# Two late gates of a decoder trunk: z times (1 + tanh(z/2)), halved later, in place of z times sigmoid(z)

## The chip, the cores and the metric

The kernel runs on one core of a Trainium2 chip. The metric is the device time of one execution in microseconds (us). Four compute engines work side by side, each with its own queue that is executed in order: TensorE (PE: matmuls and transposes), VectorE (DVE), ScalarE (ACT: copies, casts and activation functions) and GpSimd (POOL). SyncE (SP) only issues transfers here. Engines wait for one another through semaphores. Matmul results land in PSUM, everything else is in SBUF.

## The reference

A decoder trunk of one layer, for 1024 tokens of width 1024, all in float32: three groups of attention heads side by side, an output projection, a gated MLP with a convolution, a gated embedding and a last norm. The change touches the third group, retention, whose output is gated:

```
def _retention(q, k, v, g, cos, sin):
    ...
    o = _unchunk(o)
    o = _rmsnorm(o) * jax.nn.silu(g.astype(jnp.float32))
    return o.reshape(b, s, -1)
```

silu(g) is g times sigmoid(g). The first group (HGRN2) gates its output in the same way. The second group, attention in a window of 128 tokens, needs exponentials for its softmax.

## The kernel before, in words

Every matmul of float32 operands is split into high and low parts: `mm3` (lines 113 to 117) issues three matmuls, on lines 115, 116 and 117. `split_w` makes the two parts of a weight tile: ACT casts the high part (line 102), the engine named by `e` subtracts to get the low part (line 104).

The input projection has 22 column tiles of 128 columns. `project` computes one of them: a tile is a pair of PSUM banks, one for each half of the tokens (`z_cg` and the like, tag `g`, three banks in all). A function `post` then takes the two banks to SBUF, which frees them. `mixed_in` interleaves, in program order, the steps of one head group with those of the projections that follow, and the tile framework's scheduler orders each engine's queue from that program by priorities and its own estimates; so a changed instruction can move others.

The last such stage is the windowed attention (`window`, 32 steps: four pairs of heads i, two heads hd of a pair, four steps of two token blocks). A step has three pieces. `first`: score matmuls (`sb`, lines 605 and 606), masks (609, 610), the maximum (612, 613), two exponentials on ACT with their sum (line 617, tiles `pr` and `bden`). `second`: two transposes of the exponentials (`tb`, line 625), a copy of them on ACT (627) and a masked copy on DVE (628), both into `pT`. `third`: products with the values (`pob`, lines 640 and 641); at the last step of a head the sums are completed (`es` 646, `bden` 647, 648) and the output scaled (649). `heads` prepares the queries of a pair (`qs`: a cast on ACT, line 748, a subtraction on DVE, line 749).

Beside this stage run the last five projections, named in LATE: bq1, bq2, bq3 and the two retention gates cg0 and cg1. Their post for the gates is `gate` (lines 313 to 319): line 290 scales a bank by the row norms into `cg` in SBUF, ACT writes sigmoid(cg) back into the freed bank (317), DVE multiplies the two (318), and after that the bank is free. The two gates of the first head group, ag0 and ag1, went the same way in earlier stages, where no exponentials are computed.

ACT holds one set of function tables at a time. Where an activation needs another set, an instruction ACT_TABLE_LOAD stands before it. In this stage exponentials and sigmoids alternate.

The first two tiles of the output projection (`o`, `out_tile_half`, lines 823 to 827) already start in this stage; they need PSUM banks of the same tag `g`, the second one the bank of the first half of cg1. Their first operands are `ha` and `la`, the high and low part of the first group's gated output: `split` casts `ha` on ACT (line 379), and GpSimd subtracts to `la` (line 380). Both go into buffers that the projection's inputs held, so they wait until PE has used those inputs in cg1.

After the stage, `gated` turns each retention output by transposes (`gc`) and multiplies it with its gate (line 392 without a gain, line 394 with a column of gains, as for the first head group), and `split` makes the two parts `hc` and `lc`.

Of the kernel before, what the change touches and what calls it, by code (L numbers as in the profile page):

```python
# [21 lines left out]
AF = mybir.ActivationFunctionType  # L22
ALU = mybir.AluOpType
# [19 lines left out]
LATE = ("bq1", "bq2", "bq3", "cg0", "cg1")  # L43
# [30 lines left out]
def trunk(ctx: ExitStack, tc: tile.TileContext, a, out, out_end, dbg):  # L74
    nc = tc.nc
    V, S, G, TE = nc.vector, nc.scalar, nc.gpsimd, nc.tensor
# [6 lines left out]
    def dump(name, t):  # L83
        if name in dbg:
            nc.sync.dma_start(dbg[name], t.bitcast(F32) if t.dtype == F32R else t)

    def pg(name):
        return ps.tile([P, H2], F32, tag="g", bufs=3, name=name)

    def b1(name):  # L90
        return ps.tile([P, H2], F32, tag="b1", bufs=5, name=name)

    def half(h):
        return slice(h * H2, (h + 1) * H2)
# [112 lines left out]
    pt = b1("idle")  # L207
# [3 lines left out]
    with tc.high_priority(offset=100000):  # L211
# [4 lines left out]
        for k in range(KD):  # L216
# [10 lines left out]
            for h in range(2):  # L227
                S.mul(hi[:, half(h)], x[:, half(h)], col(C_G1 + k))
                V.scalar_tensor_tensor(out=lo[:, half(h)], in0=x[:, half(h)], scalar=col(C_G1 + k),
                                       in1=hi[:, half(h)].bitcast(F32), op0=ALU.mult, op1=ALU.subtract)  # L230
# [57 lines left out]
    def scaled(dst, o):  # L288
        for h in range(2):
            V.tensor_tensor(out=dst[:, half(h)], in0=o[h], in1=rs1[:, half(h)], op=ALU.mult)  # L290

    def zt(name, tag, bufs):
        return ap.tile([P, T], F32, tag=tag, bufs=bufs, name=name)

    def plain(o, name, tag, bufs):
        t = zt(name, tag, bufs)
        scaled(t, o)
        return t

    def transposed(src, name, evac):  # L300

        for h in range(2):
            pt = b1(f"{name}{h}")
            for c in range(4):
                TE.transpose(pt[:, chunk(c)], src[:, chunk(h * 4 + c)], ident)
            evac(h, pt.rearrange("p (c d) -> p c d", c=4))
# [5 lines left out]

    def gate(o, name):

        g = plain(o, name, "zg", 4)
        for h in range(2):
            S.activation(o[h], g[:, half(h)], AF.Sigmoid)
            V.tensor_tensor(out=g[:, half(h)], in0=o[h], in1=g[:, half(h)], op=ALU.mult)
        return g
# [54 lines left out]
    def split(src, gain, name, e=V, parts=1):  # L374
        hi, lo = [big.tile([P, T], F32R, tag="big", name=x + name) for x in "hl"]
        for i in range(parts):
            c = slice(i * T // parts, (i + 1) * T // parts)
            if gain is None:
                S.copy(hi[:, c], src[:, c])
                e.tensor_tensor(out=lo[:, c], in0=src[:, c], in1=hi[:, c].bitcast(F32), op=ALU.subtract)  # L380
            else:
                S.mul(hi[:, c], src[:, c], gain)
                V.scalar_tensor_tensor(out=lo[:, c], in0=src[:, c], scalar=gain, in1=hi[:, c].bitcast(F32),
                                       op0=ALU.mult, op1=ALU.subtract)
        return hi, lo

    def gated(zo, g, gain, name):

        def evac(h, pt):
            gv = g[:, half(h)].rearrange("p (c d) -> p c d", c=4)  # L390
            if gain is None:
                V.tensor_tensor(out=gv, in0=pt, in1=gv, op=ALU.mult)
            else:
                V.scalar_tensor_tensor(out=gv, in0=pt, scalar=gain, in1=gv, op0=ALU.mult, op1=ALU.mult)
        transposed(zo.rearrange("p c d -> p (c d)"), "g" + name, evac)
        dump("mix" + name, g)
        return g
# [12 lines left out]
    def hgrn_f(j, of):  # L410
        f = zt(f"f{j}", "zf", 1)
        k = zt(f"k{j}", "zk", 2)
        scaled(f, of)
        S.activation(k, f, AF.Sigmoid, scale=-1.0)
        S.activation(f, f, AF.Sigmoid)
        V.tensor_scalar(out=k, in0=k, scalar1=oml[:, j:j + 1], scalar2=None, op0=ALU.mult)
        V.tensor_scalar(out=f, in0=f, scalar1=oml[:, j:j + 1], scalar2=lbt[:, j:j + 1], op0=ALU.mult, op1=ALU.add)
        return f, k
# [244 lines left out]
    def window_out(i, zo):  # L663
        hi = big.tile([P, T], F32R, tag="big", name=f"hmb{i}")
        lo = big.tile([P, T], F32R, tag="big", name=f"lmb{i}")

        def evac(h, pt):
            pt = pt.rearrange("p c d -> p (c d)")
            S.copy(hi[:, half(h)], pt)
            V.tensor_tensor(out=lo[:, half(h)], in0=pt, in1=hi[:, half(h)].bitcast(F32), op=ALU.subtract)  # L670
        transposed(zo.rearrange("p c d -> p (c d)"), f"mb{i}", evac)
        dump(f"mixb{i}", hi)
        return hi, lo
# [4 lines left out]
    got = {}  # L678
# [16 lines left out]
    def gates(n):  # L695
        return keep(n, lambda o: gate(o, n))

    def out_tile(n, tag="zo"):
        return ap.tile([P, NC, P], F32, tag=tag, bufs=1, name=n)
# [6 lines left out]
    def mix_tile(name, z, gate, gain):  # L706

        mix[name] = gated(z, got[gate], gain, name)
        yield 0.9

    v = plain(first[2], "ai0", "zt", 1)
    f, k = hgrn_f(0, first[0])
# [5 lines left out]
    f, k = got["af1"]  # L718
# [5 lines left out]
    zc = [out_tile(f"oc{j}", ("zo", "zF")[j]) for j in range(2)]  # L724
# [34 lines left out]
             tiles_of(rot("bq1", "zq"), rot("bq2", "zq"), rot("bq3", "zq"), gates("cg0"), gates("cg1")), 0.82, 8.0)  # L759
    mh = [split(mix[n], None, n, G) for n in ("a0", "a1")]  # L760
    mh += [window_out(i, zb[i]) for i in range(4)]
    mh += [split(gated(zc[j], got[f"cg{j}"], None, f"c{j}"), None, f"c{j}") for j in range(2)]
    att.__exit__(None, None, None)
    fp = ctx.enter_context(tc.tile_pool(name="ffn", bufs=1))
    dp = ctx.enter_context(tc.tile_pool(name="spill", bufs=1, space=bass.MemoryType.DRAM))
# [103 lines left out]
    for n, (h, i, d) in enumerate((h, i, d) for h in range(2) for i in range(2) for d in range(4)):  # L869
        hi, lo = wpp[i]  # L870
        o = pg(f"pp{n}")
# [319 lines left out]
    got = {}  # L1191
    bank = {}
    todo = []
    for n, (i, j) in enumerate(steps):
# [14 lines left out]
        if j == NJ - 1:  # L1209
            d0, h = TO[i]  # L1210
# [23 lines left out]
    c = half(0)  # L1234
# [37 lines left out]
    for n in range(NC // 2):  # L1272
# [7 lines left out]
        for i, (d0, d1) in enumerate(groups):  # L1280
# [4 lines left out]
            o = pg(f"pe{n}{i}")[:, :d1 - d0]  # L1285
# [12 lines left out]
            else:  # L1298
                V.scalar_tensor_tensor(out=v[:, 3:4], in0=v[:, i:i + 1], scalar=1.0 / D, in1=v[:, 3:4],
                                       op0=ALU.mult, op1=ALU.add)  # L1300
# [3 lines left out]
        if not last:  # L1304
# [6 lines left out]
                               op1=ALU.mult)  # L1311
# [116 lines left out]
```

## Time and profile before

| | |
|---|---|
| median of three runs | 1246.35 us (1245.96 to 1246.54) |
| the profiled execution, own time | 1246.38 us |
| its span, first to last instruction | 1244.6 us |
| PE busy | 1225.4 us (98%) |
| DVE busy | 892.2 us (72%) |
| ACT busy | 543.8 us (44%) |
| POOL busy | 126.7 us (10%) |

The span is that of the profiled execution; 1.8 us of its own time lie outside it. The shares are means over the whole program. PE's matmuls are pipelined: each is listed with 0.39 us, but the next starts about 0.23 us after it, so the starts tell more than the durations.

### The profile page before, as it was taken

What the parts mean: (1) busy time and instruction counts of PE and PEld (TensorE: products, weight loads), DVE (VectorE), ACT (ScalarE), POOL (GpSimd) and SP (SyncE); (2) the same over time, 40 slices, a digit from 0 to 9 for tenths busy, and PEclk for the clock granted to TensorE, in tenths of its full rate; (3) what the DMA queues carried; (4) which work ended last, traced back from release to release, by engine and by line L of the source; (5) the groups of instructions that cost most, each with busy time, mean ns of one, the idle gap of its engine ahead of it and who ended that gap; (6) DMA issues with size and microseconds to landing.
All of it is one profiled execution on the core that took longest, in us unless ns stands there. A gap on an engine that the chain in (4) does not pass through costs nothing.

```text
span 1244.6 us, 15889 instructions
## 1 busy us (share of the span) xinstructions
PE 1225.4 (98%) x6030; PEld 1023.5 (82%) x6030; DVE 892.2 (72%) x1510; ACT 543.8 (44%) x838; POOL 126.7 (10%) x158
## 2 busy tenths in 40 slices
PE   9999999999999999999999999999999999999997
PEld 7888888887888888887788888888888888888886
DVE  7996967557777476987878887787667675566374
ACT  7324233247766344754343334433335353444332
POOL 2000000011210313100111111111101000000000
PEclk9999999999999999999999999999999999999999
DMA  7100110110001944333554544544579786443131
GB/s 258 51 23 29 35 34 18 34 34 34 24 29 46 353 127 166 121 94 127 177 177 152 179 130 154 182 160 154 191 265 339 272 290 207 144 152 119 34 135 68
DMA packets 59964, 165.53 MB, mean 133 GB/s; under 512 B 6320, under 2 KB 6832, under 8 KB 59888
## 3 DMA queue, kind: packets, MB, share of 16 engines
q1 hardware_dynamic: 42608, 106.71, 25.6%
q0 software_dynamic: 15552, 55.84, 13.2%
q10 hardware_dynamic: 1728, 1.97, 0.5%
q8 instruction: 47, 0.77, 0.3%
q14 instruction: 29, 0.24, 0.1%
HBM read 120.20 MB, written 44.30 MB: 132 GB/s over the span
## 4 chain that ended last, share of the span: by engine, by line
PE 51%; DVE 1%; DMA 0%; issue 0%; ACT 0%; DVEq 0%
PE d L116 6%; PE d L115 6%; PE d L117 6%; PE gb L116 5%; PE gb L117 5%; PE gb L115 5%; PE gd L117 3%; PE gd L115 3%; PE gd L116 3%; PE ga L116 1%; PE ga L117 1%; PE ga L115 1%; PE pe L117 1%; PE pg L115 1%; PE pe L115 1%; PE pe L116 1%
## 5 line engine op out<-in xcount | busy, mean ns | idle before, releaser
L115 PE MATMUL d<-hhd,hwd 128*128 128x512 f32 x308 | 119.8, 389 | 0.0
L116 PE MATMUL d<-lhd,hwd 128*128 128x512 f32 x308 | 119.8, 389 | 0.0
L117 PE MATMUL d<-hhd,lwd 128*128 128x512 f32 x308 | 119.8, 389 | 0.0
L781 DVE TENSOR_TENSOR lwd<-wdr,hwd 128x1024 fp32r<-128x1024 f32 (+1 forms) x39 | 47.0, 1209 | 36.9 <-ACT hwd L780 36.8
L780 ACT CAST hwd<-wdr 128x1024 fp32r<-128x1024 f32 (+1 forms) x39 | 40.5, 1039 | 72.8 <-PE d L116 59.0
L115 PE MATMUL gd<-b,f 128*128 128x512 f32 x176 | 68.8, 391 | 1.4 <-ACT us L964 1.4
L115 PE MATMUL gb<-b,hf 128*128 128x512 f32 x176 | 68.7, 390 | 0.1
L116 PE MATMUL gd<-b,f 128*128 128x512 f32 x176 | 68.5, 389 | 0.0
L117 PE MATMUL gd<-b,f 128*128 128x512 f32 x176 | 68.5, 389 | 0.0
L116 PE MATMUL gb<-b,hf 128*128 128x512 f32 x176 | 68.5, 389 | 0.0
L117 PE MATMUL gb<-b,lf 128*128 128x512 f32 x176 | 68.3, 389 | 0.0
L115 PEld LDWEIGHTS d<-hhd,hwd 128*128 128x128 f32 x308 | 57.8, 188 | 12.1
L117 PEld LDWEIGHTS d<-hhd,lwd 128*128 128x128 f32 x308 | 57.8, 188 | 12.1
L116 PEld LDWEIGHTS d<-lhd,hwd 128*128 128x128 f32 x308 | 57.8, 188 | 11.8
L781 DVE TENSOR_TENSOR lhd<-hr,hhd 128x1024 fp32r<-128x1024 f32 (+1 forms) x39 | 46.7, 1207 | 6.7 <-ACT hhd L780 6.5
L780 ACT CAST hhd<-hr 128x1024 fp32r<-128x1024 f32 (+1 forms) x39 | 39.8, 1034 | 20.1 <-DMA hr<-tad 11.0
L780 ACT CAST f<-wg 128x512 fp32r<-128x512 f32 x22 | 13.7, 624 | 77.7 <-PE gd L117 77.7
L781 DVE TENSOR_TENSOR f<-s,f 128x1024 fp32r<-128x1024 f32 x22 | 26.9, 1224 | 28.3 <-ACT f L780 28.3
L780 ACT CAST f<-s 128x1024 fp32r<-128x1024 f32 x22 | 23.1, 1050 | 50.3 <-PE gb L117 46.5
L115 PEld LDWEIGHTS gd<-b,f 128*128 128x128 f32 x176 | 33.0, 188 | 9.3 <-ACT us L964 2.5
L115 PEld LDWEIGHTS gb<-b,hf 128*128 128x128 f32 x176 | 33.0, 188 | 7.7 <-ACT gs L964 0.5
L971 DVE SCALAR_TENSOR_TENSOR cv<-gs,small,cv 128x1023 f32<-128x1023 f32 x22 | 28.2, 1284 | 15.1 <-ACT cv L970 15.1
(491 smaller groups left out, 3506.1 us busy)
## 6 DMA issues: line engine op xcount, KB each, us to landing
wg<-w_gu SPq DMA_DIRECT2D x22, 512.0 KB, 4.4
wu<-w_gu SPq DMA_DIRECT2D x22, 512.0 KB, 3.5
sd<-w_dn POOLq DMA_DIRECT2D x22, 512.0 KB, 5.2
sd<-sd POOLq DMA_DIRECT2D x22, 512.0 KB, 3.9
wdr<-sd SPq DMA_DIRECT2D x44, 256.0 KB, 3.7
wr_wo<-w_out SPq DMA_DIRECT2D x16, 512.0 KB, 3.7
wdr<-w_dn SPq DMA_DIRECT2D x15, 512.0 KB, 4.8
hod<-us POOLq DMA_DIRECT2D x11, 512.0 KB, 2.9
```

Of the source, the lines that this page charges most:

```text
L115: TE.matmul(o, wh, xh, start=first, stop=False, skip_group_check=on)
L116: TE.matmul(o, wh, xl, start=False, stop=False, skip_group_check=on)
L117: TE.matmul(o, wl, xh, start=False, stop=last, skip_group_check=on)
L780: S.copy(hi, src)
L781: return e.tensor_tensor(out=lo, in0=src, in1=hi.bitcast(F32), op=ALU.subtract)
L971: V.scalar_tensor_tensor(out=cv[:, 1:], in0=gs[:, :T - 1], scalar=w(1), in1=cv[:, 1:], op0=ALU.mult, op1=ALU.add)
```

## The change

The two gates cg0 and cg1 are computed as z (1 + tanh(z/2)), which is twice silu(z). The factor one half comes in where the turned retention output is multiplied with the gate, by a constant gain of 0.5. The other two gates stay.

```
     def gate(o, name):
 
+
         g = plain(o, name, "zg", 4)
         for h in range(2):
+            if name in LATE:
+                S.activation(o[h], g[:, half(h)], AF.Tanh, scale=0.5)
+                V.scalar_tensor_tensor(out=g[:, half(h)], in0=o[h], scalar=1.0, in1=g[:, half(h)], op0=ALU.add,
+                                       op1=ALU.mult)
+                continue
             S.activation(o[h], g[:, half(h)], AF.Sigmoid)
             V.tensor_tensor(out=g[:, half(h)], in0=o[h], in1=g[:, half(h)], op=ALU.mult)
         return g
...
             gv = g[:, half(h)].rearrange("p (c d) -> p c d", c=4)
-            if gain is None:
-                V.tensor_tensor(out=gv, in0=pt, in1=gv, op=ALU.mult)
-            else:
-                V.scalar_tensor_tensor(out=gv, in0=pt, scalar=gain, in1=gv, op0=ALU.mult, op1=ALU.mult)
+            V.scalar_tensor_tensor(out=gv, in0=pt, scalar=gain, in1=gv, op0=ALU.mult, op1=ALU.mult)
...
-    mh += [split(gated(zc[j], got[f"cg{j}"], None, f"c{j}"), None, f"c{j}") for j in range(2)]
+    mh += [split(gated(zc[j], got[f"cg{j}"], 0.5, f"c{j}"), None, f"c{j}") for j in range(2)]
```

The compiled program has six ACT_TABLE_LOADs fewer, all in this stage: the three before the sigmoids (line 317) and three of the four before exponentials (line 617). The queues of POOL and SP keep their order. Those of ACT, DVE and PE change from the first of these gates to the end of the stage. Line numbers behind the gate grow by 3 (behind `gated`, the later code too).

ACT's queue around the second half of cg0, before the change (the number behind a name is a buffer's; pr and es belong to the head being computed, qs to the next pair):

```order
L627 COPY pT_3101<-tb_3100 128x256
L317 ACT_TABLE_LOAD
L317 ACTIVATE z_cg_2920<-cg_3082 128x512
L748 CAST qs_3110<-bq_2844 64x1024
L617 ACT_TABLE_LOAD
L617 ACTIVATE pr_3090,bden_2988<-sb_3089,bmx_2987 128x128 x2
L748 CAST qs_3110<-bq_2844 64x1024
L627 COPY pT_3131<-tb_3130 128x256
L646 ACTIVATE es_3181<-bmx_2987,sink 128x8
L379 CAST ha_3382<-ag_866 128x1024
L379 CAST ha_3386<-ag_1452 128x1024
L617 ACTIVATE pr_3119,bden_3117<-sb_3118,bmx_3116 128x128 x2
```

The same place after the change:

```order
L630 COPY pT_3101<-tb_3100 128x256
L319 ACTIVATE z_cg_2920<-cg_3082 128x512
L751 CAST qs_3110<-bq_2844 64x1024 x2
L385 CAST ha_3382<-ag_866 128x1024
L620 ACTIVATE pr_3090,bden_2988<-sb_3089,bmx_2987 128x128 x2
L649 ACTIVATE es_3181<-bmx_2987,sink 128x8
L385 CAST ha_3386<-ag_1452 128x1024
L630 COPY pT_3131<-tb_3130 128x256
L620 ACTIVATE pr_3119,bden_3117<-sb_3118,bmx_3116 128x128 x2
```

The two loads are gone, the casts of qs stand together, and the casts of ha have moved ahead of the exponentials and of the copy into pT_3131.

DVE's queue a little later, before the change (bmx is the maximum that the next exponentials wait for):

```order
L609 TENSOR_TENSOR sb_3118<-sb_3118,wmask 128x128
L610 COPY_PREDICATED sb_3118<-lmask,sb_3118 128x128
L610 COPY_PREDICATED sb_3160<-lmask,sb_3160 128x2x128
L749 TENSOR_TENSOR qs_3110<-bq_2844,qs_3110 64x1024
L612 TENSOR_REDUCE sb_3118<-sb_3118 128x2
L628 TENSOR_TENSOR pT_3131<-tb_3130,tmask 128x256
L613 TENSOR_SCALAR bmx_3116<-sb_3118,nsink 128x2
L612 TENSOR_REDUCE sb_3160<-sb_3160 128x2
L647 TENSOR_TENSOR bden_2988<-bden_2988,es_3181 128x8
```

The same place after the change:

```order
L752 TENSOR_TENSOR qs_3110<-bq_2844,qs_3110 64x1024 x2
L612 TENSOR_TENSOR sb_3118<-sb_3118,wmask 128x128
L650 TENSOR_TENSOR bden_2988<-bden_2988,es_3181 128x8
L613 COPY_PREDICATED sb_3118<-lmask,sb_3118 128x128
L631 TENSOR_TENSOR pT_3131<-tb_3130,tmask 128x256
L615 TENSOR_REDUCE sb_3118<-sb_3118 128x2
L613 COPY_PREDICATED sb_3160<-lmask,sb_3160 128x2x128
L616 TENSOR_SCALAR bmx_3116<-sb_3118,nsink 128x2
```

Both subtractions of qs now stand together, and the addition into bden has moved ahead of pT_3131 and of the first bmx.

PE's queue between the scores sb_3160 and the products with pT_3131, after the change:

```order
L609 MATMUL sb_3160<-kl_2273,qs_3110 128x256
L116 MATMUL z_cg_3147<-xl_171,wh_cg_3142 128x512
L117 MATMUL z_cg_3147<-xh_170,wl_cg_3144 128x512
L115 MATMUL z_cg_3146<-xh_205,wh_cg_3142 128x512
L643 MATMUL pob_3066<-vd,pT_3131 128x64
L644 MATMUL pob_3066<-vb,pT_3131 128x64
```

Three matmuls of cg1 stand between them. Before the change there are twelve, up to `z_cg_3147<-xh_234,wh_cg_3142`; the other nine have moved behind.

## Rows read from the trace of the kernel before

**Rows 1.** Page, part 1: busy time (share of the span) and instructions of each engine.
```profile
PE 1225.4 (98%) x6030; PEld 1023.5 (82%) x6030; DVE 892.2 (72%) x1510; ACT 543.8 (44%) x838; POOL 126.7 (10%) x158
```

**Rows 2.** The core's span and mean granted clock.
```profile
core 0: 1244.6 us, clock 0.998
```

**Rows 3.** Windows, 340 to 410 us: length, busy time (instructions) by engine, clock, DMA.
```profile
340.00:410.00 70.00, 68.40 (x428) 59.21 (x427) 49.78 (x110) 43.80 (x115) 7.31 (x4) 1.00 0.20 63
```

**Rows 4.** Waits of PE, whole span: total us, times, longest.
```profile
PE gd L115 <- ACT us L964: 1.4, 2, 0.9
...
PE o L115 <- DVE cg L318: 1.3, 1, 1.3
```

**Rows 5.** Groups on ACT: count | busy us, mean ns | idle before.
```profile
L617 ACT ACT_TABLE_LOAD x4 | 5.1, 1283 | 0.8 <-DVE bmx L613 0.8
...
L317 ACT ACT_TABLE_LOAD x3 | 3.8, 1283 | 0.1
```

**Rows 6.** Timeline, ACT, at cg1: start us, duration us, line, instruction.
```profile
384.27 1.28 ACT L317 ACT_TABLE_LOAD   x1
385.56 1.12 ACT L317 ACTIVATE z_cg<-cg 128x512 f32<-128x512 f32 x2
```

**Rows 7.** Timeline, DVE, at cg1 ([...] is idle time before and its releaser).
```profile
382.74 0.68 DVE L290 TENSOR_TENSOR cg<-z_cg,rs 128x512 f32<-128x512 f32 x1
...
384.72 0.42 DVE L610 COPY_PREDICATED sb<-lmask,sb 128x256 f32<-128x256 uint8 x1
...
386.20 1.29 DVE L318 TENSOR_TENSOR cg<-z_cg,cg 128x512 f32<-128x512 f32 x2 [0.34 <-ACT z_cg L317]
```

**Rows 8.** Timeline, PE, at the first output projection.
```profile
385.23 0.39 PE L117 MATMUL o<-ha,wl_wo 128*128 128x512 f32 x1
386.94 0.50 PE L115 MATMUL o<-ha,wh_wo 128*128 128x512 f32 x1 [1.33 <-DVE cg L318]
```

**Rows 9.** Lines 318, 394 and 516: ns min/median/max, first and last start.
```profile
L318 DVE TENSOR_TENSOR cg<-z_cg,cg x4: 681/686/692, 352.8 to 386.8; 128x512 f32<-128x512 f32 x4
L394 DVE SCALAR_TENSOR_TENSOR ag<-ga,small,ag x4: 743/748/752, 134.6 to 208.5; 128x512 f32<-128x512 f32 x4
L516 DVE SCALAR_TENSOR_TENSOR ang<-angn,ang x4: 1220/1224/1227, 38.0 to 51.6; 128x1024 f32<-128x1024 f32 x4
```

**Rows 10.** Timeline, POOL and DVE, at 267 and at 369 us.
```profile
266.81 2.39 POOL L104 TENSOR_TENSOR wl_bq<-wr_bq,wh_bq 128x1024 fp32r<-128x1024 f32 x1 [80.50 <-ACT wh_bq L102]
266.93 2.29 DVE L140 SCALAR_TENSOR_TENSOR hy<-rq_t,hy 128x8 f32<-128x8 f32 x1
...
368.34 4.72 POOL L380 TENSOR_TENSOR la<-ag,ha 128x1024 fp32r<-128x1024 f32 x2 [25.40 <-ACT ha L379]
369.64 1.11 DVE L647 TENSOR_TENSOR bden<-bden,es 128x8 f32<-128x8 f32 x1
```

**Rows 11.** Timeline, ACT, second half of cg0.
```profile
360.55 1.28 ACT L317 ACT_TABLE_LOAD   x1
361.85 0.60 ACT L317 ACTIVATE z_cg<-cg 128x512 f32<-128x512 f32 x1
362.39 1.03 ACT L748 CAST qs<-bq 64x1024 fp32r<-64x1024 f32 x1
...
367.23 1.98 ACT L379 CAST ha<-ag 128x1024 fp32r<-128x1024 f32 x2
```

**Rows 12.** Timeline, DVE, the same stretch.
```profile
363.45 1.22 DVE L749 TENSOR_TENSOR qs<-bq,qs 64x1024 fp32r<-64x1024 f32 x1 [0.27 <-ACT qs L748]
...
368.85 0.42 DVE L628 TENSOR_TENSOR pT<-tb,tmask 128x256 f32<-128x256 f32 x1
```

**Rows 13.** Timeline, PE, the same stretch.
```profile
366.59 0.40 PE L116 MATMUL z_cg<-xl,wh_cg 128*128 128x512 f32 x1
...
369.34 0.43 PE L640 MATMUL pob<-vd,pT 128*128 128x64 f32 x2
...
371.51 0.68 PE L625 MATMUL tb<-ident,pr 128*128 128x128 f32 x2
```

## The prediction

> **What bounds the kernel now.** I read the page's busy times first: PE works for 1225.4 of 1244.6 us, DVE for 892.2 and ACT for 543.8 [rows 1], at a mean granted clock of 0.998 [rows 2], which is the upper of its two levels (2.4 GHz). So work taken from ACT is worth only the time in which PE waits for it. Next, the stretch that holds the changed gates: from 340 to 410 us PE is busy for 68.40 of 70.00 us [rows 3]. So 1.60 us is the idle time that this stretch can give back, and the clock there is already 1.00. Then PE's waits: over the whole span there is one of 1.3 us by `o` for DVE's line 318, the product of the gate, and a pair of 1.4 us together by `gd` in the MLP, which the change doesn't touch [rows 4]. The 1.3 us is most of the 1.60 us, and the change stands right in its chain. Last, the timelines of the three engines around it.
>
> **The gate of cg1, a gain.** The reader is to see this chain: DVE scales the second bank from 382.74 for 0.68 us [rows 7]; ACT loads a table at 384.27 for 1.28 us and the two sigmoids run from 385.56 [rows 6]; DVE's product starts at 386.20 after 0.34 us of idle time for ACT [rows 7]; PE, whose last matmul in front of this began at 385.23, goes on at 386.94, with 1.33 us of listed wait [rows 8]. It needs the bank of the first half. Without the load the first tanh starts at 384.27 and, at half of the pair's 1.12 us, ends at 384.83. DVE is not free then: its masked copy runs from 384.72 to 385.14 [rows 7], and in the new order the product stands right behind it. So DVE becomes what is late next: product from 385.14, 0.69 us [rows 9], end 385.83. In the trace PE follows the first product's end (386.20 + 0.69 = 386.89) by 0.05 us, so it would go on at 385.88 instead of 386.94: a gain of 1.06 us. The other 0.27 us of the listed wait stays.
>
> Six loads of 1.283 us go, 7.7 us of ACT [rows 5]. The other five stand where PE has matmuls of cg0 and cg1 to do and lists no wait for a gate; I count them at nothing directly, since that cover stays, and look at what they trigger instead (below).
>
> The Trainium skill (ScalarE: Activation LUTs, section "What ACT_TABLE_LOAD costs") gives 1283 ns for the load and about 1380 ns for a drain, 2.66 us for a switch. By that six switches would be 16 us of ACT, and the gate of cg1 would come free another 1.4 us earlier on ACT's side, which would still end at DVE's masked copy, so the sum stays. The trace has the load, and the sigmoid 1.29 us after its start [rows 6]; no drain is seen there.
>
> **The new operations.** No tanh runs in this trace. Sigmoids of that shape take 0.60 us alone and 0.56 in the pair [rows 6, 11]. I take 0.56; as bounds a tanh of a quarter less costs or gives nothing, because DVE is late, and one of twice the time (1.12) would end at 385.39 and cost 0.25 us at cg1. The new product on DVE has a constant as scalar. With a column as scalar the same shape takes 748 ns, against 686 for the plain product; with a constant it took 1224 ns for twice the columns [rows 9], 0.61 us by halving. I take 0.69; the bounds 0.61 to 0.75 move PE's restart at cg1 by -0.08 to +0.06 us. The four products with the turned outputs (line 392) change in the same way, 0.06 us each at most, 0.25 us on DVE; the matmuls of `hmb` hide them, and uncovered they would cost that 0.25 us. The halving itself adds no instruction.
>
> **What moves, a loss.** Here the change isn't just a deletion. Without the load at 360.55, ACT does tanh (0.60) and both casts of qs (1.03 each), and then the first cast of ha, which now starts near 363.1 instead of 367.23 [rows 11] and ends near 364.1. GpSimd's subtraction `la`, 2.37 us each (two in 4.72), follows it 4.2 us earlier than at 368.34 [rows 10]. That matters since GpSimd's subtractions hold up some DVE instructions: an addition of 8 columns into bden took 1.11 us and ended at 370.75, just as the first `la` was over (368.34 + 2.37 = 370.71); another tiny instruction took 2.29 us beside the GpSimd instruction at 266.81 and ended with it, at 269.22 [rows 10]. Both have two operands in SBUF. In the new order DVE has three such instructions close together: the two subtractions of qs (1.22 us each [rows 12]), from about 363.0 to 365.4, and then the addition into bden, which now stands in front of the masked copy, pT_3131 and bmx.
>
> PE meanwhile comes to the products with pT_3131 earlier. Before, twelve matmuls lie between 366.59 and 369.34, 0.229 us each [rows 13]; three are left, so PE arrives at 366.59 + 0.69 = 367.28. In the old trace pT_3131 is done at 368.85 + 0.42 = 369.27 [rows 12], just in time for 369.34.
>
> The likeliest course: the second subtraction of qs starts before GpSimd gets going, `la` runs from about 365.3 to 367.7, and bden, issued once the scores sb_3118 are there (shortly before 366.59), ends at 367.7. Behind it the masked copy and pT_3131 take at most 0.42 us each: 368.5 less some overlap, 368.4. PE waits 368.4 - 367.3 = 1.1 us. In return the wait of the old order goes: the pair of transposes at 371.51 took 0.68 us [rows 13], in which PE waited for exponentials behind the held bden; with the gap ahead of it I put this at 0.5 us, an estimate.
>
> The Trainium skill (GPSIMD Engine Reference, section "Specifications") says that GpSimd shares its SBUF interfaces with VectorE and contends with DVE instructions that have two SBUF inputs. By it the masks and pT, which read PSUM, would pass, and only qs and bden be held, as I have it; were every DVE instruction held, the wait of 1.1 us would grow by up to 2.4. The two held rows of 267 and 369 us agree with it; whether it is the same at 364 us no trace of before shows.
>
> **Sum.** -1.06 (gate) + 1.1 (held bden) - 0.5 (old wait) = -0.46 us. From the profiled execution's own 1246.38 us (span 1244.6 and 1.8 outside, 0.03 above the median of the runs) that is 1245.9 us. What follows slides along: from there on PE lists no wait but the `gd` pair [rows 4], whose chain starts from PE's own results.
>
> **Rivals.**
> - GpSimd first: slower than before. `la` is ready near 364.1, in the middle of the two subtractions of qs. If it gets in before the second, that one waits until 366.5 and ends at 367.7; the second `la` then runs from 367.7 to 370.1, and bden, again held, ends at 370.1, pT_3131 at 370.8. PE waits 3.5 us: -1.06 + 3.5 - 0.5 = +1.9, 1248.3 us. For it: in rows 10 GpSimd, once started, ends first each time. Against it: the two subtractions stand back to back in DVE's queue, and the margin is some tenths of a us. It decides from `la` running ahead of the second qs.
> - No collision: bden is through before `la` starts or PE's wait is covered. Then -1.06 - 0.5 = -1.6, 1244.8 us; with every bit of the stretch's 1.60 us of idle time and the 0.5 it would be 1244.3. Against it: `la` lasts 4.7 us from 364.1 or later, and bden falls into that.
> - Nothing gained: the bank of cg1 is released as late as before, because the first tanh finds ACT behind with something else or DVE's masked copy late. 1246.4 us, with the losses above smaller too, since all is then as in the old order. Against it: ACT goes from the exponentials straight into the load at 384.27.
> - The change doesn't do what it says, tanh needing a table of its own: excluded, the loads are gone from the compiled queue.
>
> **Numbers.** Forecast 0.45, GpSimd first 0.25, no collision 0.20, nothing gained 0.10. The range: the forecast with its tanh and product bounds and the estimate of 0.5 at nothing reaches from 1245.3 to 1246.7; the range takes in no collision down to 1244.2 and GpSimd first up to 1248.4. A measurement of this kernel can tell 0.2%, 2.5 us, from no change. Faster by that needs less than 1243.9, which the waits at hand hardly hold: 0.03. Slower by that needs more than 1248.8, GpSimd first with both held a little longer: 0.07. Within: 0.90.
>
> **What would show it.** Right: no wait of `o` on the gate above 0.4 us; a line 650 (bden) of about 1 us beside `la`, which starts near 364 to 365; a wait of about 1 us of PE before `pob` near 367; no stretched pair of transposes near 371. A second subtraction of qs listed with over 3 us is the first rival. The forecast is wrong if PE still waits over 1 us for the gate, if bden is not held at all, or if time changes outside 350 to 400 us.

## The result and the profile after

The changed kernel takes 1250.26 us (median of ten runs; before on the same chip 1246.56), ratio 1.0030 with a 95% interval of 1.0022 to 1.0038. One of the ten ran in a slow state (2061.03 us at a mean granted clock of 0.555) and doesn't enter the ratio; the median of the other nine is 1249.81. By the ratio the kernel is slower by 3.7 us; 1245.9 was forecast, and the time lies above the range. The profiled execution took 1249.81 us, 3.43 more than that of before, and 3.4 of it are in the span (1248.0 against 1244.6 [rows 2]).

Waits of PE in the whole span (us in total, times, longest), which answer to [rows 4]:

```profile
PE pob L643 <- DVE pT L631: 4.0, 3, 3.1
...
PE o L115 <- DVE cg L320: 0.2, 1, 0.2
```

The gate's wait went from 1.3 to 0.2 us, as forecast. A new one of 3.1 us stands at the top: pob for pT. The windows around it show what came with it (length, busy time of PE, PEld, DVE, ACT and POOL with their instructions, granted clock, DMA share, GB/s):

```profile
355.00:367.00 12.00, 12.00 (x78) 10.81 (x78) 9.67 (x15) 8.30 (x19) 2.52 (x2) 1.00 0.14 44
367.00:370.50 3.50, 0.69 (x3) 0.20 (x2) 3.47 (x5) 0.00 (x0) 3.16 (x1) 1.00 0.00 0
370.50:376.00 5.50, 5.23 (x26) 4.63 (x27) 3.14 (x11) 2.25 (x10) 0.00 (x0) 0.69 0.00 1
```

From 367 to 370.5 PE works for 0.69 us, while DVE and POOL are busy for almost all of it; behind that the granted clock is 0.69 in the mean of 5.5 us. The timeline of DVE in this stretch (start, duration), answering to [rows 12], and the spread of the two subtractions qs (ns min/median/max, first and last start):

```profile
363.28 4.67 DVE L752 TENSOR_TENSOR qs<-bq,qs 64x1024 fp32r<-64x1024 f32 x2
367.99 0.30 DVE L612 TENSOR_TENSOR sb<-sb,wmask 128x128 f32<-128x128 f32 x1
368.20 1.99 DVE L650 TENSOR_TENSOR bden<-bden,es 128x8 f32<-128x8 f32 x1
370.11 0.28 DVE L613 COPY_PREDICATED sb<-lmask,sb 128x128 f32<-128x128 uint8 x1
370.30 0.41 DVE L631 TENSOR_TENSOR pT<-tb,tmask 128x256 f32<-128x256 f32 x1
```
```profile
L752 DVE TENSOR_TENSOR qs<-bq,qs x2: 1219/2322/3425, 363.3 to 364.5; 64x1024 fp32r<-64x1024 f32 x2
```

The timeline of POOL and the spread of its two subtractions, answering to [rows 10]:

```profile
364.48 5.68 POOL L386 TENSOR_TENSOR la<-ag,ha 128x1024 fp32r<-128x1024 f32 x2 [21.27 <-ACT ha L385]
```
```profile
L386 POOL TENSOR_TENSOR la<-ag,ha x2: 2400/2862/3325, 364.5 to 366.8; 128x1024 fp32r<-128x1024 f32 x2
```

Read the two engines together. The first qs takes its 1.22 us and ends at 364.50; the first la starts at 364.48, 0.05 us ahead of the second qs (363.28 + 4.67 - 3.425 = 364.53). That qs stands in the record for 3.425 us, 2.2 more than the first: it is over 1.07 us after the first la (367.95 against 364.48 + 2.40 = 366.88). The second la in turn is held until qs is done, 3.325 us instead of 2.40. Then bden, which has 8 columns, comes to 368.20 and is held to the end of the second la (370.16). So the two engines take turns, one instruction each, and pT starts at 370.30 instead of 368.85. The addition of wmask at 367.99 has one operand in PSUM and ran in 0.30 us in the middle of the second la.

PE's timeline at the hole and behind it, answering to [rows 13]:

```profile
367.29 0.40 PE L115 MATMUL z_cg<-xh,wh_cg 128*128 128x512 f32 x1
370.77 0.44 PE L643 MATMUL pob<-vd,pT 128*128 128x64 f32 x2 [3.08 <-DVE pT L631]
...
372.30 0.63 PE L117 MATMUL z_cg<-xh,wl_cg 128*128 128x512 f32 x1
372.73 0.63 PE L115 MATMUL z_cg<-xh,wh_cg 128*128 128x512 f32 x1
```

After 3.08 us without work the matmuls of z_cg start 0.43 us apart, where before it was 0.229 [rows 13]: the lower level, 1.2 GHz. By the window it costs (1 - 0.69) x 5.50 = 1.7 us. Last, the gate of cg1, PE and then ACT and DVE, answering to [rows 6 to 8]:

```profile
389.79 0.39 PE L117 MATMUL o<-ha,wl_wo 128*128 128x512 f32 x1
390.41 0.50 PE L115 MATMUL o<-ha,wh_wo 128*128 128x512 f32 x1 [0.23 <-DVE cg L320]
```
```profile
388.76 1.12 ACT L319 ACTIVATE z_cg<-cg 128x512 f32<-128x512 f32 x2
```
```profile
389.33 0.42 DVE L613 COPY_PREDICATED sb<-lmask,sb 128x256 f32<-128x256 uint8 x1
389.66 1.28 DVE L320 SCALAR_TENSOR_TENSOR cg<-z_cg,cg 128x512 f32<-128x512 f32 x2
```

From start to start PE needs 0.62 us across the gate instead of 1.71: 1.09 us gained. Counted in the same way, the hole costs 370.77 - 367.29 - 0.23 = 3.25 us (3.08 is the listed wait, which begins only at the end of the matmul before it). Two smaller terms belong to the sum. The old wait of transposes near 371 is gone; an experiment below measures it at 0.76. And this execution was already 0.27 us later ahead of everything that moved: the same matmul of cg0 starts at 339.49 in the trace of before and at 339.76 here. The sum of the rows: -1.09 (gate) + 3.25 (hole) + 1.7 (clock) - 0.76 (old wait) + 0.27 = 3.37, against 3.43 measured.

### The profile page after: what moved, and what is told of

It is laid out like the page before. It is cut to its first block, busy times and chain, and to the rows that moved or that the text cites. A ratio compares the mean times of both kernels' runs of the same rounds, so it can differ in the third digit from the quotient of the medians.

```text
span 1248.0 us, 15885 instructions
## 1 busy us (share of the span) xinstructions
PE 1227.9 (98%) x6030; PEld 1025.2 (82%) x6030; DVE 894.4 (72%) x1510; ACT 535.6 (43%) x832; POOL 127.6 (10%) x158
## 4 chain that ended last, share of the span: by engine, by line
PE 51%; DVE 1%; DMA 0%; issue 0%; ACT 0%; DVEq 0%
PE d L116 6%; PE d L117 6%; PE d L115 6%; PE gb L117 5%; PE gb L115 5%; PE gb L116 5%; PE gd L115 3%; PE gd L117 3%; PE gd L116 3%; PE ga L117 1%; PE ga L115 1%; PE ga L116 1%; PE pe L117 1%; PE pg L115 1%; PE pe L115 1%; PE pe L116 1%
```

## The experiments

Theory A: the casts ha, and behind them GpSimd's la, run early; la holds the second qs and bden on DVE, pT is late, PE idles for 3 us and then runs at the lower clock. Rivals: B, the order on PE (three matmuls left to cover pT instead of twelve); C, the new operations themselves; D, a lower clock that has nothing to do with the idle time; E, bden alone is held; F, the order of the casts is worth more than the gates. Four kernels ran on one chip (before: 1246.52 us), four on another (1246.47).

### The casts held back, the tanh gates kept

```
+    exps = {}
...
+                x = S.activation(pr[:, u, :], sm[:, u, :], AF.Exp, bias=mx[:, n:n + 1], scale=0.125,
+                                 accum_out=den[:, n:n + 1])
+                exps[i, hd, n] = x
...
+    with tc.issue_after(exps[3, 0, 3].ins):
+        mh = [split(mix[n], None, n, G) for n in ("a0", "a1")]
```

> The changed kernel, with the two casts of the mixers' rows to ha (and so GpSimd's subtractions la) held in the order of issue behind the exponentials of pair 3, block 3; the two tanh gates stay. DVE, TensorE and the gates keep the changed kernel's order around the stall (three matmuls of z_cg stand between the scores and the last output matmuls of pair 2, as in the changed kernel). Theory A (GpSimd's subtractions, now early, hold VectorE's two-operand subtractions qs and the sum bden, TensorE idles 3.1 us for pT and then runs at a lower clock): the wait of pob for pT falls from 3.1 us to under 0.5, the qs pair takes 2.4 us instead of 4.67, bden 0.2 instead of 1.99, the clock stays at 1.00 in the stretch behind it, and only the gate's gain of 1.1 us and the old wait of 0.5 are left: 1244.9 us, ratio to before 0.9987 (0.998 to 0.9995). Rival B (the new order on TensorE, three matmuls instead of twelve ahead of those output matmuls, makes it wait whatever GpSimd does): the wait stays at 2 to 3 us, 1248 to 1250. Rival C (the new operations, tanh and the three-operand multiply, cost it): 1249 to 1250.

Measured: 1244.08 us, ratio 0.9979 (0.9969 to 0.9988). DVE, POOL, and the window of 340 to 410 us, which answers to [rows 3]:

```profile
363.38 2.47 DVE L755 TENSOR_TENSOR qs<-bq,qs 64x1024 fp32r<-64x1024 f32 x2
...
366.64 0.16 DVE L653 TENSOR_TENSOR bden<-bden,es 128x8 f32<-128x8 f32 x1
```
```profile
371.52 4.74 POOL L386 TENSOR_TENSOR la<-ag,ha 128x1024 fp32r<-128x1024 f32 x2 [28.31 <-ACT ha L385]
```
```profile
340.00:410.00 70.00, 69.71 (x436) 60.68 (x435) 50.38 (x113) 37.62 (x112) 8.46 (x6) 1.00 0.22 70
```

With la at 371.5 the qs pair takes 2.47 us and bden 0.16, PE waits for nothing there, with the same three matmuls in between, and the clock is 1.00. That contradicts B and C. PE is busy for 69.71 of the 70 us (68.40 before), and this is the fastest of all kernels here, 2.4 us below before, 0.8 better than A expected.

The traces show where the 0.8 lies. Between one matmul of cg0 near 339 us and the last of cg1, PE does the same 270 matmuls in both kernels, only in another order. Before (the row of 386.94 stands in [rows 8]):

```profile
339.49 0.39 PE L117 MATMUL z_cg<-xh,wl_cg 128*128 128x512 f32 x1
...
382.26 0.39 PE L117 MATMUL z_cg<-xh,wl_cg 128*128 128x512 f32 x1
```

With the casts held back:

```profile
339.75 0.39 PE L117 MATMUL z_cg<-xh,wl_cg 128*128 128x512 f32 x1
...
381.67 0.39 PE L117 MATMUL z_cg<-xh,wl_cg 128*128 128x512 f32 x1
...
384.88 0.50 PE L115 MATMUL o<-ha,wh_wo 128*128 128x512 f32 x1
```

The stretch takes 41.92 us instead of 42.77, 0.85 less, where A had 0.5 for the old wait. From its end to the matmul behind the gate it is 3.21 us instead of 4.68, 1.47 less, where A had 1.1: PE's wait at the gate is gone altogether. Together 2.3 of the 2.4 us.

### The subtractions la on DVE

```
-    mh = [split(mix[n], None, n, G) for n in ("a0", "a1")]
+    mh = [split(mix[n], None, n, V) for n in ("a0", "a1")]
```

> The changed kernel, with the subtractions la on VectorE instead of GpSimd; the casts ha stay early. GpSimd then does nothing in the stretch, VectorE has two more instructions of 1.22 us (one of them between bden and pT), and eight matmuls of z_cg stand between the scores and the output matmuls instead of three. Theory A: qs pair 2.4 us, bden 0.2, pT by about 368.3, TensorE reaches the output matmuls at about 368.8 and waits under 0.5 us, no fall of the clock: 1245.0 us, up to 1246.3 if the second la delays a later tile; ratio 0.9987 to 1.0000. Rival B (too few matmuls in between): eight times 0.23 instead of three times 0.23 hides 1.15 us, wait 2 us, 1248 to 1249. Rival C (the new operations): 1249 to 1250.

Measured: 1245.72 us, ratio 0.9991 (0.9982 to 1.0000). The first cast of ha is early here too (363.23 us, 363.35 in the changed kernel), but GpSimd is out of it:

```profile
363.15 2.47 DVE L752 TENSOR_TENSOR qs<-bq,qs 64x1024 fp32r<-64x1024 f32 x2
366.41 0.16 DVE L650 TENSOR_TENSOR bden<-bden,es 128x8 f32<-128x8 f32 x1
```

Neither is held, PE lists no wait for pT in this stretch, and 4 to 5 us of the changed kernel's time are gone (ratio 0.9991 against 1.0030). So it is GpSimd that holds DVE, not the early cast on ACT.

### One gate at a time

```
-            if name in LATE:
+            if name == "cg1":
```

(the other kernel has "cg0" there; the gain of 0.5 goes with that gate alone)

> Only the second late gate (cg1) by tanh; the first keeps its sigmoid and its plain multiply. The order around pair 2's output matmuls is then that of before: the casts ha after es, twelve matmuls of z_cg in between. Theory A: no early GpSimd, no stall; the gate's gain alone (TensorE's wait for cg at 387 falls from 1.33 to about 0.25 us): 1245.4 us, ratio 0.9991 (0.9985 to 0.9997). Rival C (the new operations cost it): 1247.5 to 1248, half of the loss.

> Only the first late gate (cg0) by tanh; the second keeps its sigmoid. The order around pair 2's output matmuls is that of the changed kernel: casts ha early, three matmuls in between, bden ahead of pT. Theory A: the whole stall (3.1 us) and the lower clock behind it, and without the second gate's gain of 1.1 us: 1251.2 us, ratio 1.0038 (1.003 to 1.005). Rival C (the new operations cost it): 1247.5 to 1248. If the loss hung on the second gate: 1246.4.

Measured: cg1 alone 1245.26 us, 0.9988 (0.9979 to 0.9997); cg0 alone 1251.10 us, 1.0037 (1.0025 to 1.0049). With cg1 alone, PE's only wait from 355 to 395 us:

```profile
PE o L115 <- DVE cg L320: 0.2, 1, 0.2
```

With cg0 alone, PE's waits in the same stretch, DVE's qs pair, and the window behind the hole:

```profile
PE pob L646 <- DVE pT L634: 3.1, 1, 3.1
PE o L115 <- DVE cg L324: 1.4, 1, 1.4
```
```profile
363.30 4.68 DVE L755 TENSOR_TENSOR qs<-bq,qs 64x1024 fp32r<-64x1024 f32 x2
```
```profile
370.50:376.00 5.50, 5.21 (x25) 4.60 (x26) 3.13 (x11) 2.24 (x10) 0.00 (x0) 0.69 0.01 1
```

The change falls into two parts: the second gate brings 1.3 us, the first costs 4.6 (1251.10 - 1246.52), with the same hole and the same lower clock as in the changed kernel. Both use the same new operations, which again speaks against C.

### The changed kernel without bden's sum

```
+                if (i, hd) != (2, 1):
                     V.tensor_tensor(out=den, in0=den, in1=es, op=ALU.add)
```

> The changed kernel without one instruction: the sum of es into bden of pair 2, second head, which stands between the qs subtractions and pT on VectorE (the sums of that head's softmax lack the sink's term). Everything else keeps the changed kernel's order. Theory A (both VectorE waits come from GpSimd's la, 2.27 us at the qs pair and 1.8 us at bden; the clock falls because TensorE was idle for 3 us): the qs pair still takes 4.67 us, pT starts at about 368.5 instead of 370.3, TensorE's wait for it falls from 3.1 to about 1.3 us, and after so short an idle the clock stays at 1.00 (as it did after the 1.33 us idle at 385 of the kernel before): 1250.3 - 1.8 - 1.7 = 1246.8 us, ratio to before 1.0002 (0.999 to 1.001). Rival D (the lower clock has nothing to do with the length of the idle time): 0.69 again in the stretch behind, 1248.5. Rival E (bden alone is held, the qs pair not): no wait left, 1244.5.

Measured: 1246.03 us, ratio 0.9998 (0.9989 to 1.0007). DVE, PE and the window behind the hole:

```profile
362.93 4.68 DVE L753 TENSOR_TENSOR qs<-bq,qs 64x1024 fp32r<-64x1024 f32 x2
```
```profile
368.65 0.43 PE L643 MATMUL pob<-vd,pT 128*128 128x64 f32 x2 [1.31 <-DVE pT L631]
```
```profile
370.50:376.00 5.50, 5.50 (x42) 4.87 (x40) 3.69 (x12) 3.42 (x16) 0.00 (x0) 1.00 0.01 4
```

The qs pair is held as before, which contradicts E; PE's wait is 1.31 us instead of 3.08, and the clock stays up, which contradicts D. Taking away 1.77 us of wait made the kernel some 4 us faster (ratio 0.9998 against 1.0030): more than the wait itself, and near the 1.77 + 1.7 us of wait and clock together.

### Work for PE in the hole

```
+            if (i, hd, n0) == (2, 1, 6):
+                for _ in range(12):
+                    TE.matmul(po[:, 384:512], pT[:, 1, 0, :], ident, start=True, stop=True)
```

(the transposes of the next scores are issued behind pob's matmuls)

> The changed kernel with 12 matmuls of 128 columns put between the scores and pob's waiting matmuls of pair 2, into columns of pob that the waiting matmuls write anew (work that nothing uses); they start when ScalarE's half of pT is there. VectorE and GpSimd collide as before, but TensorE has work in the hole. Three matmuls of z_cg that stood there come later (0.7 us), and the next transposes may wait for their exponentials. Theory A with the clock falling on TensorE's idle time: idle time in one piece falls from 3.1 us to about 1.0, pob still starts at about 370.7, and the granted clock of the stretch behind stays at 1.00 instead of 0.69; of the saving of about 1.7 us the moved matmuls and the wait for the exponentials take 0.7 to 2 back: 1249.2 to 1250.6 us. Rival D (the clock falls for another reason): 0.69 again, 1251 to 1252.

Measured: 1249.57 us, ratio 1.0025 (1.0015 to 1.0036). PE and the window behind:

```profile
367.09 2.94 PE L641 MATMUL pob<-ident,pT 128*128 128x128 f32 x24
370.90 0.43 PE L646 MATMUL pob<-vd,pT 128*128 128x64 f32 x2 [0.87 <-DVE pT L631]
```
```profile
370.50:376.00 5.50, 4.85 (x30) 4.07 (x31) 4.02 (x14) 2.84 (x14) 0.00 (x0) 1.00 0.02 4
```

pob starts as late as in the changed kernel (370.90), DVE and GpSimd collide as there (the second qs takes 3.43 us), but the granted clock is 1.00: the fall came from PE's idle time, not from the collision. The time is inside what A expected, but it doesn't show the price of the clock: the times of this and of the changed kernel overlap within their intervals. The matmuls moved behind the hole (0.7 us) take part of what the clock gives back; what takes the rest was not measured.

### The sigmoid kept, only the casts moved

Late, as in the first experiment:

> The kernel before, both late gates by their sigmoid, with only the order of the casts ha changed: held behind the exponentials of pair 3, block 3. Asks how much of the 2.4 us that the same order gave beside the tanh gates belongs to the order alone. In the kernel before, la held the sum bden of pair 2 for 1 us (1.11 instead of 0.17), and TensorE waited about 0.5 us behind it. Theory A: bden takes 0.17 us, that wait goes, the gate's wait of 1.33 us stays: 1246.0 us, ratio 0.9996 (0.999 to 1.0000). Rival F (the late casts free something larger, and the tanh gates give nothing with it): 1244.1 to 1244.8.

Early, by a priority:

```
+    with tc.high_priority(offset=300):
+        mh = [split(mix[n], None, n, G) for n in ("a0", "a1")]
```

> The kernel before, both late gates by their sigmoid, with the casts ha moved early by a higher priority: no tanh anywhere. ScalarE now has ha ahead of the qs casts of pair 3, so these come 2 us later; three matmuls of z_cg stand ahead of pob's, bden ahead of pT, as in the changed kernel. Theory A (an early GpSimd subtraction costs it, whatever the gates are): the qs pair is held by la and takes over 3.5 us instead of 2.4, TensorE waits 2 us or more for pT or for the scores, and the time rises without any tanh: 1249 to 1252 us. Rival C (it needs the new operations): 1246 to 1247.

Measured, late: 1246.35 us, 0.9997 (0.9988 to 1.0006). bden takes 0.16 us and the gate's wait stays, and the time is far from the 1244.1 to 1244.8 that F wants, so F falls. In the time of the whole program the later casts alone bring nothing that can be told from zero. DVE, PE's waits from 355 to 395 us, and the two ends of the same 270 matmuls:

```profile
369.79 0.16 DVE L650 TENSOR_TENSOR bden<-bden,es 128x8 f32<-128x8 f32 x1
```
```profile
PE o L115 <- DVE cg L318: 1.3, 1, 1.3
```
```profile
339.62 0.39 PE L117 MATMUL z_cg<-xh,wl_cg 128*128 128x512 f32 x1
...
381.63 0.39 PE L117 MATMUL z_cg<-xh,wl_cg 128*128 128x512 f32 x1
```

The stretch itself does show something: 42.01 us instead of 42.77, 0.76 less. That is the old wait behind the held bden, measured alone in one trace.

Measured, early: 1251.08 us, 1.0040 (1.0026 to 1.0053), from four executions that lie far apart (1249.32 to 1253.85). The time is what A expected, the reason is not. The qs pair was held by 1.02 us (3.49 instead of 2.47), but PE had matmuls of z_cg to do, and its longest waits lie elsewhere:

```profile
367.64 3.49 DVE L749 TENSOR_TENSOR qs<-bq,qs 64x1024 fp32r<-64x1024 f32 x2 [4.28 <-ACT qs L748]
```
```profile
PE tb L625 <- ACT pr L617: 1.4, 1, 1.4
PE o L115 <- DVE cg L318: 0.8, 1, 0.8
...
```

Here ACT's casts of qs come late as well (4.28 us of idle time on DVE for them), so this run shows that early casts of ha can cost as much without tanh, but not by the way of the changed kernel. The wait of 1.4 us stands at 388.4 us, after the last matmul of z_cg (379.05, before 382.26); how the rest comes about stays open.

## Why the prediction was wrong

- **The gate of cg1** was right: 1.06 us forecast, 1.09 in the trace, 1.3 us (0.4 to 2.6 by its interval) in the kernel with cg1 alone. DVE's masked copy and product end last there, and 0.23 us of wait stays, as worked out (0.27).
- **The new operations** were right: a pair of tanh takes 1.12 us, a pair of products with the constant 1.28 us, as the sigmoids and the plain products did [rows 6, 7].
- **What moves** holds the step that failed. The move was seen: ha early, la from about 364, qs and bden as the instructions at risk. The choice between the two courses was wrong: "the second subtraction of qs starts before GpSimd gets going". In the trace la starts 0.05 us ahead of it. The kernel with cg0 alone has the same order and margin, 364.51 for la and 364.55 for the second qs. So the rival "GpSimd first" is what happened, with pT's end at 370.71 (370.30 + 0.41), where its working had 370.8. The prediction's own times spoke for that rival: with la ready near 364.1 and the first qs from about 363.0 to 364.2, la was not behind, and yet the forecast let it start only at 365.3. In [rows 10], too, the GpSimd instruction had started first both times, and the one on DVE ended with it. Nothing in the rows gave the other course the larger chance (0.45 against 0.25).
- **The price of that rival** was too low. It had +1.9 us; the profiled execution has +3.43. What lies between them, 1.5 us, is the lower clock after the hole (1.7), which the prediction put at nothing in every case, less 0.25 because the hole was 3.25 us and not 3.5. In the trace of before, PE's wait of 1.33 us at the gate [rows 8] left the clock at 1.00. Its only fall stands at the very end, where PE has been without work since its last matmul, which started at 1235.13 (the window's row, columns as above):

```profile
1240.00:1244.60 4.60, 0.00 (x0) 0.00 (x0) 0.51 (x1) 0.48 (x1) 0.00 (x0) 0.53 0.29 114
```

So that trace showed that idle time of PE can cost the clock, but not from what length on; a forecast with a hole of 3.5 us had to name the risk.
- **The old wait** of 0.5 us was an estimate, and it was somewhat low: the kernel with the sigmoid and late casts, which removes bden's hold, does the same 270 matmuls 0.76 us faster in its trace. Its time as a whole can't tell (0.1 us faster, interval from 1.5 faster to 0.7 slower).

The held rows mean an exclusive resource: one instruction has it to its end, the other waits, in both directions (qs 3.425 us, la 3.325). The Trainium skill (SBUF — State Buffer, section "Who interferes with whom") has this as a rule: a VectorE instruction with two SBUF inputs and a GpSimd instruction that reads SBUF can't run together, and the one that issues first holds the shared ports for the whole instruction. The trace agrees, and the addition at 367.99, with one operand in PSUM, was not held; by that rule too the start decided, and the two starts were 0.05 us apart.

## What to carry to other kernels

Removing ACT instructions lets what is queued behind them run early, and here the early part, a GpSimd subtraction, cost over three times what the removal gained (4.6 against 1.3 us); look for what the freed engine triggers before counting the gain, and if it collides, hold it back in the order of issue (1244.08 us with the same gates). Where two engines race for one resource and the margin is below what the rows can tell, give neither course the larger chance. A stall of PE that is longer than any stall whose clock the trace shows is to be forecast with and without a lower clock behind it.

## What the runs showed of the hardware

- GpSimd's and DVE's subtractions and additions with both operands in SBUF exclude each other for whole instructions, and both wait: qs 3.425 us instead of 1.219, la 3.325 instead of 2.400, bden (8 columns) 1.99 instead of 0.16.
- PE's granted clock was at its lower level after idle time of 3.08 us (changed kernel, and with cg0 alone); after 1.31 us (without bden's sum) and 0.87 us (with the filling matmuls) it stayed at 1.00. What lies between was not tried. The fall cost 1.7 us by the window; with the hole shortened to 1.31 us the whole kernel was some 4 us faster.
